# The normalisation stage of an encoder layer, written out by hand in each engine's order

## The chip, the core and the metric

The kernel runs on one core of a Trainium2 chip. A core has five engines that work side by side, each through its own queue of instructions: TensorE (PE in the profile; its loads of weights are PEld), VectorE (DVE), ScalarE (ACT), GpSimd (POOL) and SyncE (SP). They wait for each other by semaphores. Transfers between memory and the core are run by 16 DMA engines; SyncE, ScalarE and GpSimd can issue them. The metric is the device time of one execution in microseconds.

## The reference

The kernel computes one layer of a hybrid encoder (`DEPTH` is 1) on 512 tokens of width 2048, with 16 learned meta tokens ahead of them, so 528 rows in all. What the change touches is the first step, the RMS norm, and two of the column groups of the projection behind it:

```python
def rmsnorm(x, w):
    xf = x.astype(jnp.float32)
    y = xf * lax.rsqrt(jnp.mean(xf * xf, axis=-1, keepdims=True) + EPS)
    return (y * w.astype(jnp.float32)).astype(x.dtype)
...
    u = rmsnorm(h, norm_w)
    proj = u @ w_in.astype(dt_)
...
    gcode = gcode.reshape(Bsz, L, 2, GLA_RANK).astype(jnp.float32)
...
    dt = jax.nn.softplus(dt_raw.reshape(Bsz, L, 2, SSD_HEADS).astype(jnp.float32)
                         + ssd_dt_bias.astype(jnp.float32))
...
    o_gla = rmsnorm(o, gla_norm_w).astype(dt_).reshape(Bsz, L, GLA_WIDTH) * jax.nn.silu(ggate)
```

All other column groups of `proj` feed three branches (gated linear attention, differential attention, a state-space scan), whose outputs go through one output projection, a residual and a last norm.

## The kernel before, in words

The rows of the input are five blocks: `xt[4, j]` the 16 meta tokens, `xt[0, j]` to `xt[3, j]` 128 tokens each, and each block is four pieces j of 512 columns. `normalize(t)` squares the four pieces, some on ScalarE and some on VectorE, sums the squares (`ss`), takes the root on GpSimd (`r`) and scales the pieces in place. `features` then turns each of the 16 feature tiles k: transposes on TensorE into `pb`, one copy to `uh` on ScalarE (times `norm_w`), and the rest of each value, `ul`, on VectorE. A value is thus kept as two parts, so that a product of full precision is three matmuls (`uh` with `whi`, `ul` with `whi`, `uh` with `wlo`). `whi` and `wlo` are the two parts of a weight; a copy on ScalarE and a subtraction on VectorE make them.

Two groups of products stand in this stage: B, 48 matmuls for each half of the rows (`t1_half`; the first half is the blocks 4, 0, 1, the second the blocks 2, 3), and the small group of the codes and of dt, `comb` (`comb_half`), 32 for each half. There are four `pb` buffers. Behind the stage comes a chain on `comb` that gives dt and the decays (up to `Xr`), and the products of the next column tiles.

The order of before is not written by hand. The framework's scheduler takes the instructions of the whole kernel and orders them on each engine by its own model of their times; so an instruction that stands late in the source can come early in a queue. Each engine takes its queue in order. Loads use eight counters in turn: a load is issued only when the one that used its counter before, eight loads ahead, has landed.

`gn` holds the norm weights of two branches, each loaded broadcast to 128 partitions (L304, L305) and scaled on VectorE (L306, L307). It is first read 464.8 us into the span (L883).

Of the kernel before, what the change touches and what calls it, by code (L numbers as in the profile page):

```python
# [8 lines left out]
F32 = mybir.dt.float32  # L9
# [8 lines left out]
P = 128  # L18
# [24 lines left out]
def encoder_kernel(ctx, tc, x, meta, rel_bias, final_norm_w, norm_w, w_in, w_out, gla_wa2, gla_ba,  # L43
# [27 lines left out]
    def cpy(out, in_, **kw):  # L71
        nc.scalar.activation(out, in_, AF.Copy, **kw)  # L72
# [78 lines left out]

    def t1_weights(c0, nk, tag):

        out_ = []
        for k0 in range(0, KT, 8):
            raw = wpool.tile([P, 8, P], F32, name="wraw")
            nc.sync.dma_start(raw, win[:, k0:k0 + 8, c0:c0 + P])
            for i in range(0, 8, nk):
                hi = slot(tag, [P, nk, P], F32R, name="whi")
                lo = slot(tag, [P, nk, P], F32R, name="wlo")  # L160
                cpy(hi, raw[:, i:i + nk])
                tt(lo, raw[:, i:i + nk], hi.bitcast(F32), ALU.subtract)
                out_.append((hi, lo))
        return out_

    def t1_half(acc, ws, hf):
        nk = KT // len(ws)
        o, us = (acc[0][:, 0:HA], slice(0, HA)) if hf == 0 else (acc[1][:, 0:HB], slice(HA, L))
        for k in range(KT):
            hi, lo = ws[k // nk]  # L170
            for n, (wt, ur) in enumerate(((hi, uh[k]), (hi, ul[k]), (lo, uh[k]))):
                mm(nc, o, wt[:, k % nk, :], ur[:, us], k == 0 and n == 0, k == KT - 1 and n == 2)
# [73 lines left out]
    nc.tensor.transpose(pv[:, 0:92], vecs, ident[0:92, 0:92])
    nc.vector.tensor_copy(vt, pv[:, 0:92])
    nw = vt[:, 0:16]
    gba = vt[:, 88:92]

    def normalize(t):
        rows = NM if t == 4 else P
        ss = small.tile([P, 1], F32, name="ss")
        ssq = small.tile([P, 5], F32, name="ssq", bufs=5)
        nc.gpsimd.memset(ssq[:, 4:5], EPS)
        for j in range(4):
            scr = slot("w")
            if j < (2 if t < 2 else 3):
                nc.scalar.activation(scr[0:rows, 0:512], xt[t, j][0:rows], AF.Square, scale=D ** -0.5,
                                     accum_out=ssq[0:rows, j:j + 1])  # L260
            else:
                nc.vector.tensor_tensor_reduce(scr[0:rows, 0:512], xt[t, j][0:rows], xt[t, j][0:rows], 1.0 / D, 0.0,
                                               ALU.mult, ALU.add, ssq[0:rows, j:j + 1])
        nc.vector.tensor_reduce(ss[0:rows], ssq[0:rows], AX.X, ALU.add)
        r = small.tile([P, 1], F32, name="r")
        gtt(r[0:rows], ss[0:rows], mhalf[0:rows, 0:1], ALU.pow)
        for j in range(4):
            if j == 3:
                cpy(xt[t, j][0:rows], xt[t, j][0:rows], scale=r[0:rows, 0:1])
            else:  # L270
                ts_(xt[t, j][0:rows], xt[t, j][0:rows], r[0:rows, 0:1], None, ALU.mult)

    def features(parts, us):
        for k in range(KT):
            pt = pb()
            n = 0
            for t in parts:

                nc.tensor.transpose(pt[:, n:n + P], xt[t, k // 4][:, (k % 4) * P:(k % 4 + 1) * P], ident)
                n += NM if t == 4 else P  # L280
            cpy(uh[k][:, us], pt[:, 0:n], scale=nw[:, k:k + 1])
            stt(ul[k][:, us], pt[:, 0:n], nw[:, k:k + 1], uh[k][:, us].bitcast(F32), ALU.mult, ALU.subtract)
# [733 lines left out]
```

## Time and profile before

| | |
|---|---|
| median of three runs | 920.37 us (917.81 to 920.91) |
| the profiled execution | 917.57 us, span 915.8 us |
| TensorE busy | 876.9 us, 96% of the span |
| VectorE busy | 554.0 us, 60% |
| ScalarE busy | 383.7 us, 42% |
| GpSimd busy | 183.7 us, 20% |
| share of the 16 DMA engines, 0 to 12 us and 12.0 to 23.1 us | 0.82 and 1.04 |

The profiled execution is one run; its span goes from the first to the last instruction, and 1.8 us lie around it. Busy matmuls are pipelined, so that one can begin while the one before it is still counted. The stage of the change is the first 54 us or so of the span.

### The profile page before, as it was taken

To read this page: it belongs to the slowest core of one execution; us is meant where nothing else is said; L and a number is where in the kernel's file an instruction comes from. 1 tells how busy PE (TensorE), PEld (TensorE's weight loads), DVE (VectorE), ACT (ScalarE), POOL (GpSimd) and SP (SyncE) were. 2 spreads that over 40 slices of the span, in tenths; PEclk is the share of its full clock that TensorE was granted. 3 is DMA by queue.
4 is the path that set the end of the run, shared out by engine and by line. 5 is a ranking of instruction groups with operands and counts; after the bars stand their busy time and mean duration, and the time that the engine had idled before them with its cause. 6 is when DMAs were issued, how large, how long until landed. Compare 5 with 4: busy or idle time off the path is not lost.

```text
span 915.8 us, 14461 instructions
## 1 busy us (share of the span) xinstructions
PE 876.9 (96%) x5737; PEld 779.9 (85%) x5737; DVE 554.0 (60%) x1049; ACT 383.7 (42%) x753; POOL 183.7 (20%) x215
## 2 busy tenths in 40 slices
PE   3898999999999999999999999999999999999996
PEld 3898999997778888899999999988888888888884
DVE  6669977999957568853642467775552543232334
ACT  6555434335534376734232345553342333132322
POOL 2006203549246302010040000000120002020200
PEclk9999999999999999999999999999999999999998
DMA  9422332221223234123337333324223532322225
GB/s 238 106 70 69 76 87 71 64 76 46 70 72 91 79 85 115 47 70 93 87 77 203 84 82 84 85 81 136 81 81 103 173 123 90 109 92 92 93 92 184
DMA packets 99587, 88.33 MB, mean 96 GB/s; under 512 B 8223, under 2 KB 75415, under 8 KB 99519
## 3 DMA queue, kind: packets, MB, share of 16 engines
q1 hardware_dynamic: 95183, 77.06, 29.8%
q0 software_dynamic: 1456, 5.10, 1.9%
q10 hardware_dynamic: 2880, 5.24, 1.7%
q8 instruction: 45, 0.74, 0.3%
q14 instruction: 23, 0.19, 0.1%
HBM read 83.18 MB, written 6.34 MB: 98 GB/s over the span
## 4 chain that ended last, share of the span: by engine, by line
PE 75%; DVE 12%; ACT 4%; issue 4%; DMA 2%; SPq 1%; POOL 1%; ACTq 0%; POOLq 0%; DVEq 0%
PE pm L39 65%; PE pb L39 7%; DVE acc L413 2%; DVE wlo L146 2%; DMA xt<-in_x_dram 2%; PE pb L898 1%; PE pb L852 1%; DVE sg L450 1%; ACT whi L72 1%; DVE acc L411 1%; DVE xs L459 1%; DMA gn<-in_diff_norm_w_dram 1%; SPq L228 1%; DVE m L552 1%; DVE m L453 0%
## 5 line engine op out<-in xcount | busy, mean ns | idle before, releaser
L146 DVE TENSOR_TENSOR wlo<-wraw,whi 128x1024 fp32r<-128x1024 f32 (+1 forms) x128 | 163.7, 1280 | 212.6 <-ACT whi L72 212.3
L72 ACT ACTIVATE whi<-wraw 128x1024 fp32r<-128x1024 f32 (+1 forms) x134 | 137.2, 1025 | 297.6 <-PE pm L39 237.4
L39 PE MATMUL pm<-ul,whi 128*128 128x272 f32 (+2 forms) x960 | 224.4, 300 | 0.0
L39 PE MATMUL pm<-uh,whi 128*128 128x272 f32 (+2 forms) x960 | 221.9, 298 | 0.6 <-ACT uh L72 0.6
L39 PE MATMUL pm<-uh,wlo 128*128 128x256 f32 (+2 forms) x928 | 214.6, 297 | 1.2 <-DVE wlo L146 0.7
L39 PEld LDWEIGHTS pm<-uh,whi 128*128 128x128 f32 x960 | 154.8, 189 | 6.7 <-ACT uh L72 1.2
L39 PEld LDWEIGHTS pm<-ul,whi 128*128 128x128 f32 x960 | 155.0, 189 | 5.1 <-issue 0.2
L39 PEld LDWEIGHTS pm<-uh,wlo 128*128 128x128 f32 x928 | 149.7, 189 | 6.8 <-DVE wlo L146 2.1
L39 PE MATMUL pm<-wlo,uh 128*128 128x512 f32 x256 | 102.5, 401 | 2.3 <-DVE wlo L146 2.3
L39 PE MATMUL pm<-whi,ul 128*128 128x512 f32 x256 | 101.3, 397 | 0.0
L39 PE MATMUL pm<-wlo,mh 128*128 128x512 f32 x256 | 100.6, 394 | 0.0
L39 PE MATMUL pm<-whi,ml 128*128 128x512 f32 x256 | 100.5, 394 | 0.0
L39 PE MATMUL pm<-whi,uh 128*128 128x512 f32 x256 | 95.0, 398 | 0.0
L39 PE MATMUL pm<-whi,mh 128*128 128x512 f32 x256 | 90.3, 395 | 0.0
L129 POOL TENSOR_TENSOR rs_r<-rs_v,mhalf 128x1 f32<-128x1 f32 (+1 forms) x28 | 20.5, 734 | 273.2 <-DVE rs_v L128 191.9
L39 PEld LDWEIGHTS pm<-wlo,uh 128*128 128x128 f32 x256 | 48.6, 190 | 13.3 <-DVE wlo L146 2.8
L39 PEld LDWEIGHTS pm<-whi,ml 128*128 128x128 f32 x256 | 48.2, 188 | 11.4
L39 PEld LDWEIGHTS pm<-whi,ul 128*128 128x128 f32 x256 | 48.6, 190 | 10.5
L39 PEld LDWEIGHTS pm<-whi,mh 128*128 128x128 f32 x256 | 48.1, 188 | 11.1
L39 PEld LDWEIGHTS pm<-wlo,mh 128*128 128x128 f32 x256 | 48.1, 188 | 10.9
L39 PEld LDWEIGHTS pm<-whi,uh 128*128 128x128 f32 x256 | 48.2, 189 | 10.7
L932 POOL TENSOR_TENSOR hx<-hx,fw 128x512 f32<-128x512 f32 x12 | 18.1, 1537 | 164.6 <-ACT junk L919 164.6
(304 smaller groups left out, 1197.7 us busy)
## 6 DMA issues: line engine op xcount, KB each, us to landing
wraw<-in_w_in_dram SPq DMA_DIRECT2D x96, 512.0 KB, 3.9
wraw<-in_w_out_dram SPq DMA_DIRECT2D x30, 512.0 KB, 3.6
xt<-in_x_dram SPq DMA_DIRECT2D x16, 256.0 KB, 5.2
hx<-in_x_dram ACTq DMA_DIRECT2D x16, 256.0 KB, 3.9
out_dram<-hx SPq DMA_DIRECT2D x16, 256.0 KB, 2.8
tabr<-tabd POOLq DMA_DIRECT2D x4, 520.0 KB, 7.0
bt<-tabr POOLq DMA_DIRECT2D x4, 456.0 KB, 3.6
fw<-in_final_norm_w_dram ACTq DMA_DIRECT2D x4, 256.0 KB, 4.3
```

Source lines behind the costliest of these rows:

```text
L39: nc.tensor.matmul(out, lhsT=lhsT, rhs=rhs, start=start, stop=stop)
L72: nc.scalar.activation(out, in_, AF.Copy, **kw)
L129: gtt(r[0:rows, 0:cols], v[0:rows, 0:cols], mhalf[0:rows, 0:cols], ALU.pow)
L146: tt(lo, raw, hi.bitcast(F32), ALU.subtract)
L228: nc.sync.dma_start(raw[:, :, 32 * i:32 * i + 32], win[:, k0:k0 + 8, c0:c0 + 32])
L411: ts_(acc, xp[:, 0:L], cw[:, 0:1], cbb[:, j:j + 1], ALU.mult, ALU.add)
L413: stt(acc, xp[:, k:k + L], cw[:, k:k + 1], acc, ALU.mult, ALU.add)
L450: stt(sg[:, c], px[:, c * P:(c + 1) * P], Xs[:, 1, c, h:h + 1], sg[:, c], ALU.subtract, ALU.min)
L459: tt(lo, src, hi.bitcast(F32), ALU.subtract)
L552: tt(m, m, sc, ALU.mult)
L852: nc.tensor.transpose(pt[:, c * P:(c + 1) * P], w_[:, c * P:(c + 1) * P], ident)
L932: gtt(hx[t, b], hx[t, b], fw[b], ALU.mult)
```

## The change

The scheduler is switched off for the stage (`tc.manual_schedule()`): its instructions stand in each engine's queue in the order in which the new code gives them. Block 0 is squared and scaled first, the transposes run three tiles ahead of the copies, and the products of `comb` follow those of B with a lag of six tiles, and one tile in the second half. The first load of B's weights and one of `comb` stand ahead of x block 2. The identity, the meta tokens and `pick` are loaded from ScalarE's queue, `norm_w`, the conv weights and two more vectors from GpSimd's. The scaling of the meta block, of block 2 and of half of block 3 goes to GpSimd. The loads and scalings of `gn` are moved down in the source, behind the gated linear attention. What stands outside the `with` is still placed by the scheduler.

```diff
-    for t in (4, 0, 1):
-        normalize(t)
-    features((4, 0, 1), slice(0, HA))
-    comb_ps, b_ps = (pm(), pm()), (pm(), pm())
-    t1_half(b_ps, b_w, 0)
-    comb_half(comb_ps, 0)
-    for t in (2, 3):
-        normalize(t)
-    features((2, 3), slice(HA, L))
-    t1_half(b_ps, b_w, 1)
-    comb_half(comb_ps, 1)
...
+    def scale(t, j, eng):
+        rows = NM if t == 4 else P
+        ap = xt[t, j][0:rows]
+        if eng == "A":
+            cpy(ap, ap, scale=rx[t][0:rows, 0:1])
+        else:
+            (nc.vector if eng == "V" else nc.gpsimd).tensor_scalar(ap, ap, rx[t][0:rows, 0:1], None, ALU.mult)
...
+    def turn(hf, k, parts):
+
+        if (hf, k) not in pts:
+            pts[hf, k] = pb()
+        n = 0
+        for t in BL[hf]:
+            if t in parts:
+
+                nc.tensor.transpose(pts[hf, k][:, n:n + P], xt[t, k // 4][:, (k % 4) * P:(k % 4 + 1) * P], ident)
+            n += NM if t == 4 else P
+
+    def parts_of_u(hf, k):
+        us, n = US[hf], (HA, HB)[hf]
+        pt = pts[hf, k]
+        cpy(uh[k][:, us], pt[:, 0:n], scale=nw[:, k:k + 1])
+        stt(ul[k][:, us], pt[:, 0:n], nw[:, k:k + 1], uh[k][:, us].bitcast(F32), ALU.mult, ALU.subtract)
+
+    def prod_b(hf, k):
+        o = b_ps[hf][:, 0:(HA, HB)[hf]]
+        hi, lo = b_w[k // 4]
+        for n, (wt, ur) in enumerate(((hi, uh[k]), (hi, ul[k]), (lo, uh[k]))):
+            mm(nc, o, wt[:, k % 4, :], ur[:, US[hf]], k == 0 and n == 0, k == KT - 1 and n == 2)
...
+    with tc.manual_schedule():
+
+        load_x(0)
+        nc.scalar.dma_start(ident, masks[M_ID])
+        nc.vector.memset(zp, 0.0)
+        for j in range(4):
+            xt[4, j] = slot("ya", [P, 512], name="mt")
+            nc.gpsimd.memset(xt[4, j], 0.0)
+            nc.scalar.dma_start(xt[4, j][0:NM], meta[:, j * 512:(j + 1) * 512])
...
+        load_x(1)
...
+        load_b()
+        load_comb()
+        load_x(2)
+        load_comb()
+        load_b()
+        load_x(3)
...
+        LEAD = 3
+        for k in range(LEAD):
+            turn(0, k, (4, 0))
...
+        scale(0, 3, "A")
+        split_b()
+        scale(1, 0, "V")
+        scale(1, 1, "A")
+        for k in range(LEAD):
+            turn(0, k, (1,))
+        todo = [lambda: scale(1, 2, "V"), lambda: split_b(), lambda: scale(1, 3, "A"),
+                lambda: split_comb(), lambda: square(2, 0, "A"), lambda: split_b(),
+                lambda: square(2, 2, "V"), lambda: square(2, 1, "A"), lambda: square(2, 3, "V"),
+                lambda: split_b(), lambda: root(2), lambda: split_comb(),
+                lambda: [scale(2, j, "P") for j in range(4)], lambda: square(3, 0, "A"),
+                lambda: square(3, 2, "V"), lambda: square(3, 1, "A"), lambda: square(3, 3, "V"),
+                lambda: root(3), lambda: [scale(3, j, "P") for j in range(2)],
+                lambda: scale(3, 2, "V"), lambda: scale(3, 3, "A")]
+        CLAG = 6
+        for k in range(KT + CLAG):
+            if k < KT:
+                parts_of_u(0, k)
+                if k + LEAD < KT:
+                    turn(0, k + LEAD, BL[0])
+                prod_b(0, k)
+            for _ in range(2):
+                if todo:
+                    todo.pop(0)()
+            if k >= CLAG:
+                prod_comb(0, k - CLAG)
+            if k >= KT + CLAG - LEAD:
+                turn(1, k - (KT + CLAG - LEAD), BL[1])
...
@@ -300,19 +376,9 @@
...
-    gn = const.tile([P, 2, P], F32, name="gn")
-    nc.sync.dma_start(gn[:, 0], gla_norm_w.broadcast_to([P, P]))
-    nc.sync.dma_start(gn[:, 1], diff_norm_w.broadcast_to([P, P]))
-    ts_(gn[:, 0], gn[:, 0], 0.5, None, ALU.mult)
-    ts_(gn[:, 1], gn[:, 1], 1.0 - LAMBDA_INIT, 0.5, ALU.mult, ALU.mult)
...
@@ -763,6 +829,12 @@
...
+    gn = const.tile([P, 2, P], F32, name="gn")
+    nc.sync.dma_start(gn[:, 0], gla_norm_w.broadcast_to([P, P]))
+    nc.sync.dma_start(gn[:, 1], diff_norm_w.broadcast_to([P, P]))
+    ts_(gn[:, 0], gn[:, 0], 0.5, None, ALU.mult)
+    ts_(gn[:, 1], gn[:, 1], 1.0 - LAMBDA_INIT, 0.5, ALU.mult, ALU.mult)
```

What the scheduler made of it is seen in the queues of the two built programs. First VectorE of the kernel before, in the first half of the stage; `ul_143` is `ul` of feature tile 7, `ul_144` of tile 8.

```order
L282 SCALAR_TENSOR_TENSOR ul_143<-pb,vt,uh_127 128x272
L306 TENSOR_SCALAR gn<-gn 128x128
L307 TENSOR_SCALAR gn<-gn 128x128
L264 TENSOR_REDUCE ss<-ssq 128x1
L282 SCALAR_TENSOR_TENSOR ul_144<-pb,vt,uh_128 128x272
L282 SCALAR_TENSOR_TENSOR ul_145<-pb,vt,uh_129 128x272
L282 SCALAR_TENSOR_TENSOR ul_146<-pb,vt,uh_130 128x272
```

And VectorE of the changed kernel at its scalings of `gn`; `ul_99` is `ul` of tile 0, `ul_100` of tile 1, `L206` a scaling of x block 1, `L222` a split of B's weights, `L237` one of `comb`'s.

```order
L260 SCALAR_TENSOR_TENSOR ul_99<-pb,vt,uh_83 128x272
L206 TENSOR_SCALAR xt<-xt,r 128x512
L222 TENSOR_TENSOR wlo<-wraw,whi 128x512
L835 TENSOR_SCALAR gn<-gn 128x128
L836 TENSOR_SCALAR gn<-gn 128x128
L260 SCALAR_TENSOR_TENSOR ul_100<-pb,vt,uh_84 128x272
L237 TENSOR_TENSOR whi<-wraw,whi 128x8x64
L260 SCALAR_TENSOR_TENSOR ul_101<-pb,vt,uh_85 128x272
L222 TENSOR_TENSOR wlo<-wraw,whi 128x512
```

The two scalings stood behind `ul` of tile 7 and stand behind `ul` of tile 0 now. Next SyncE's queue before, from x block 3 on, with the counter for which each load waits.

```order
L86 DMA xt<-in_x_dram 128x512 [waits DMAHW1_49]
L86 DMA xt<-in_x_dram 128x512 [waits DMAHW2_49]
L86 DMA xt<-in_x_dram 128x512 [waits DMAHW3_49]
L86 DMA xt<-in_x_dram 128x512 [waits DMAHW4_49]
L298 DMA umask<-in_umask_dram 128x128 [waits DMAHW5_49]
L300 DMA row_636<-in_ssd_dt_bias_dram 128x32 [waits DMAHW6_49]
L301 DMA row_636<-in_ssd_A_log_dram 128x32 [waits DMAHW7_49]
L302 DMA row_636<-in_ssd_D_dram 128x16 [waits DMAHW0_49]
L304 DMA gn<-in_gla_norm_w_dram 128x128 [waits DMAHW1_49]
L305 DMA gn<-in_diff_norm_w_dram 128x128 [waits DMAHW2_49]
L309 DMA masks<-in_masks_dram 128x4x128 [waits DMAHW3_49]
```

The same place in the changed kernel.

```order
L181 DMA xt<-in_x_dram 128x512 [waits DMAHW0_49]
L181 DMA xt<-in_x_dram 128x512 [waits DMAHW1_49]
L181 DMA xt<-in_x_dram 128x512 [waits DMAHW2_49]
L181 DMA xt<-in_x_dram 128x512 [waits DMAHW3_49]
L374 DMA umask<-in_umask_dram 128x128 [waits DMAHW4_49]
L376 DMA row_649<-in_ssd_dt_bias_dram 128x32 [waits DMAHW5_49]
L377 DMA row_649<-in_ssd_A_log_dram 128x32 [waits DMAHW6_49]
L378 DMA row_649<-in_ssd_D_dram 128x16 [waits DMAHW7_49]
L379 DMA masks<-in_masks_dram 128x4x128 [waits DMAHW0_49]
L833 DMA gn<-in_gla_norm_w_dram 128x128 [waits DMAHW1_49]
L834 DMA gn<-in_diff_norm_w_dram 128x128 [waits DMAHW2_49]
```

The load of `gn` from `diff_norm_w` shared its counter with the second piece of x block 3, and shares it with the third now; the load of the masks stood behind it and stands ahead.

## Rows read from the trace of the kernel before

**Rows 1.** The page's busy times: engine, us, share of the span, instructions.

```profile
PE 876.9 (96%) x5737; PEld 779.9 (85%) x5737; DVE 554.0 (60%) x1049; ACT 383.7 (42%) x753; POOL 183.7 (20%) x215
```

**Rows 2.** Windows: stretch in us, busy us and instructions by engine, clock, DMA, GB/s.

```profile
core 0: us, PE busy (x) PEld busy (x) DVE busy (x) ACT busy (x) POOL busy (x), PEclk, DMA share, GB/s
...
12.00:23.10 11.10, 8.82 (x35) 7.16 (x36) 9.81 (x28) 8.48 (x20) 1.45 (x4) 1.00 1.04 246
0.00:30.80 30.80, 14.21 (x78) 12.36 (x78) 18.58 (x56) 20.14 (x53) 6.74 (x24) 1.00 0.88 223
30.80:53.45 22.65, 21.93 (x180) 21.31 (x180) 13.22 (x29) 12.23 (x28) 0.37 (x3) 1.00 0.26 68
70.00:80.00 10.00, 7.14 (x55) 6.60 (x53) 9.53 (x13) 3.33 (x6) 6.23 (x5) 1.00 0.08 24
222.00:231.30 9.30, 6.46 (x27) 4.70 (x26) 9.30 (x12) 4.28 (x11) 9.14 (x6) 1.00 0.09 34
231.30:234.80 3.50, 3.50 (x11) 2.69 (x10) 3.50 (x10) 1.89 (x3) 0.35 (x1) 0.51 0.55 157
```

**Rows 3.** The chain of waits, 0 to 54 us: start, us, what.

```profile
18.22 5.96 DMA xt<-in_x_dram
24.20 5.88 DMA gn<-in_diff_norm_w_dram
```

**Rows 4.** Timeline of VectorE: start, us, instruction, idle before and its releaser.

```profile
17.92 0.49 DVE L282 SCALAR_TENSOR_TENSOR ul<-pb,vt,uh 128x272 fp32r<-128x272 f32 x1
...
26.87 0.50 DVE L282 SCALAR_TENSOR_TENSOR ul<-pb,vt,uh 128x272 fp32r<-128x272 f32 x1
27.28 0.22 DVE L306 TENSOR_SCALAR gn<-gn 128x128 f32<-128x128 f32 x1
30.10 0.23 DVE L307 TENSOR_SCALAR gn<-gn 128x128 f32<-128x128 f32 x1 [2.59 <-DMA gn<-in_diff_norm_w_dram]
```

**Rows 5.** Timeline of TensorE, around its first rise of clock and its wait.

```profile
22.07 0.43 PE L39 MATMUL pm<-uh,whi 128*128 128x272 f32 x1
...
23.27 0.29 PE L39 MATMUL pm<-uh,whi 128*128 128x272 f32 x1
...
30.85 0.33 PE L279 MATMUL pb<-masks,mt 128*128 128x128 f32 x1 [2.36 <-DVE ul L282]
```

**Rows 6.** Timeline of SyncE's queue: start and us of an issue.

```profile
23.21 0.33 SPq L304 DMA_DIRECT2D gn<-in_gla_norm_w_dram  x1
24.20 0.33 SPq L305 DMA_DIRECT2D gn<-in_diff_norm_w_dram  x1
24.84 0.38 SPq L309 DMA_DIRECT2D masks<-in_masks_dram  x1
```

**Rows 7.** Time from issue to landing of the two loads of `gn`.

```profile
DMA to landing us min/median/max: 3.3/4.6/5.9
```

**Rows 8.** Groups of VectorE, 0 to 54 us: busy us, mean ns, idle before.

```profile
L282 DVE SCALAR_TENSOR_TENSOR ul<-pb,vt,uh 128x272 fp32r<-128x272 f32 x16 | 7.4, 495 | 1.2 <-ACT uh L72 1.2
...
L262 DVE CUSTOM_DVE_ANT_0 w<-xt 128x512 f32<-128x512 f32 x6 | 4.0, 682 | 0.3 <-DMA xt<-in_x_dram 0.2
L162 DVE TENSOR_TENSOR wlo<-wraw,whi 128x512 fp32r<-128x512 f32 x4 | 2.7, 679 | 0.0
```

**Rows 9.** Groups of GpSimd over the whole span.

```profile
L883 POOL TENSOR_TENSOR od<-od,gn 128x512 f32<-128x512 f32 x4 | 5.2, 1298 | 2.1 <-DVE od L866 2.1
...
L266 POOL TENSOR_TENSOR r<-ss,mhalf 128x1 f32<-128x1 f32 x4 | 2.6, 661 | 17.8 <-DVE ss L264 17.8
...
L106 POOL MEMSET mt<- 128x1024 f32 x2 | 1.8, 950 | 0.3 <-POOLq L1002 0.3
```

**Rows 10.** Waits of TensorE over the whole span: us, times, longest.

```profile
PE pb L39 <- DVE Xr L388: 2.9, 1, 2.9
```

More of the change, by code (lines that the diff above doesn't have):

```diff
@@ L150, in encoder_kernel @@
     wout = w_out.rearrange("o (k p) c -> p (o k) c", p=P)
[L152 to L172, printed above, removed]
     def t1(cols, tokens=True):
@@ new lines, in square, with root @@
+    def square(t, j, eng):
+        rows = NM if t == 4 else P
+        scr = slot("w")
+        if eng == "A":
+            nc.scalar.activation(scr[0:rows, 0:512], xt[t, j][0:rows], AF.Square, scale=D ** -0.5,
+                                 accum_out=ssq[t][0:rows, j:j + 1])
+        else:
+            nc.vector.tensor_tensor_reduce(scr[0:rows, 0:512], xt[t, j][0:rows], xt[t, j][0:rows], 1.0 / D, 0.0,
+                                           ALU.mult, ALU.add, ssq[t][0:rows, j:j + 1])
+    def root(t):
+        rows = NM if t == 4 else P
+        ss = small.tile([P, 1], F32, name="ss")
+        nc.vector.tensor_reduce(ss[0:rows], ssq[t][0:rows], AX.X, ALU.add)
+        rx[t] = small.tile([P, 1], F32, name="r")
+        gtt(rx[t][0:rows], ss[0:rows], mhalf[0:rows, 0:1], ALU.pow)
@@ L248, in encoder_kernel @@
[L248 to L282, printed above, removed]
-    for t in (4, 0, 1):
-        normalize(t)
@@ new lines, in prod_comb @@
+    def prod_comb(hf, k):
+        o = comb_ps[hf][:, 0:(HA, HB)[hf]]
+        for n, ur in enumerate((uh[k], ul[k])):
+            mm(nc, o, comb_w[k // 8][:, k % 8, :], ur[:, US[hf]], k == 0 and n == 0, k == KT - 1 and n == 1)
+    vecs = slot("st", [92, P], name="vecs")
+    pks = slot("w", [P, 32], name="pks")
+    with tc.manual_schedule():
+        load_x(0)
+        nc.scalar.dma_start(ident, masks[M_ID])
+        nc.vector.memset(zp, 0.0)
+        for j in range(4):
+            xt[4, j] = slot("ya", [P, 512], name="mt")
+            nc.gpsimd.memset(xt[4, j], 0.0)
+            nc.scalar.dma_start(xt[4, j][0:NM], meta[:, j * 512:(j + 1) * 512])
+        nc.gpsimd.memset(mhalf, -0.5)
+        nc.vector.memset(warm, 0.0)
+        nc.scalar.activation(warm, warm, AF.Exp)
+        load_x(1)
+        for t in range(5):
+            ssq[t] = small.tile([P, 5], F32, name="ssq", bufs=5)
+            nc.gpsimd.memset(ssq[t][:, 4:5], EPS)
+        nc.gpsimd.dma_start(vecs[0:16], norm_w.rearrange("o (k p) -> (o k) p", p=P))
+        nc.gpsimd.dma_start(vecs[16:76], conv_w.rearrange("o k (j p) -> (o k j) p", p=P))
+        nc.gpsimd.dma_start(vecs[76:88], conv_b.rearrange("o (j p) -> (o j) p", p=P))
+        nc.gpsimd.dma_start(vecs[88:92].rearrange("h (z k) -> h z k", z=2),
+                            gla_ba.rearrange("o z (h k) -> (o h) z k", h=4))
+        load_b()
[4 more added lines that the diff above has]
+        load_x(3)
+        cpy(XE, zp[0:96, 0:8].rearrange("p a b -> p (a b)"))
+        cpy(BE, vz[0][0:96])
+        cpy(RB, vz[0][0:96, 0:4])
+        square(0, 0, "A")
+        square(0, 2, "V")
+        square(0, 1, "A")
+        square(0, 3, "V")
+        root(0)
+        nc.scalar.dma_start(pks, pick.rearrange("p z h -> p (z h)"))
+        pv = pb()
+        nc.tensor.transpose(pv[:, 0:92], vecs, ident[0:92, 0:92])
+        square(4, 0, "A")
+        square(4, 2, "V")
+        square(4, 1, "A")
+        square(4, 3, "V")
+        root(4)
+        nc.vector.tensor_copy(vt, pv[:, 0:92])
+        scale(0, 0, "V")
+        scale(0, 1, "A")
+        scale(0, 2, "V")
+        for j in range(4):
+            scale(4, j, "P")
+        LEAD = 3
+        for k in range(LEAD):
+            turn(0, k, (4, 0))
+        square(1, 0, "A")
+        square(1, 2, "V")
+        square(1, 1, "A")
+        square(1, 3, "V")
+        root(1)
+        scale(0, 3, "A")
[26 more added lines that the diff above has]
+                turn(1, k - (KT + CLAG - LEAD), BL[1])
+        for k in range(KT):
+            parts_of_u(1, k)
+            if k + LEAD < KT:
+                turn(1, k + LEAD, BL[1])
+            prod_b(1, k)
+            if k >= 1:
+                prod_comb(1, k - 1)
+        prod_comb(1, KT - 1)
```

84 lines of the change are left out of this document (38 added, 46 removed).

## Prediction

> **What bounds the kernel now.** I read the page first. TensorE is busy for 96% of the span [rows 1], so what a change is worth is the time in which TensorE has no product to run, or runs at half speed. The windows put most of that at the start: in the first 30.8 us TensorE issues 78 matmuls, and in the next 22.65 us it issues 180, one each 0.126 us [rows 2]. This first part is the normalisation stage. The chain of waits says what ends last there: the load of a piece of x, and right behind it the load of `gn` from `diff_norm_w`, which lands 5.88 us after its issue, at 30.08 [rows 3]. Nothing in this stage needs `gn`. The timeline of VectorE shows why it counts all the same: the scaling of `gn` stands in VectorE's queue between `ul` of feature tile 7 and `ul` of tile 8, VectorE takes its instructions in order, and it stands idle there for 2.59 us until the load lands [rows 4]. TensorE starts again at 30.85, after 2.36 us, with `ul` as its releaser [rows 5].
>
> **The change, part by part.** *What bears on nothing.* The same squares, splits, transposes and 160 products are run; so their own time is the same, and only their order and their waits are to be priced. The loads of meta tokens, identity, vectors and `pick` leave SyncE's queue. I cost that at nothing: the DMA engines are full while x comes in (share 1.04 from 12.0 to 23.1 [rows 2]), so the bytes in front of the last pieces of x take the same time. The price if that cover were gone stands with the rivals.
>
> *Where `gn` stands now.* The source moves `gn` far down, but the built program does not: its two scalings stand in VectorE's queue behind `ul` of tile 0 and ahead of `ul` of tile 1. In the trace of before VectorE had done eight `ul` when it met the load; now it will have done one. I take VectorE to be there at about 20 us: its first `ul` starts at 17.92 in before [rows 4], and one scaling and one split follow. When exactly doesn't matter as long as `gn` is later. Behind the two rows wait `ul` 1 to 15, the other splits, and the squares of x blocks 2 and 3; behind those waits TensorE. ScalarE has the like: its `ea` (from `A_log`) now stands ahead of `uh` of tile 1, but `A_log` is issued three loads ahead of the first `gn`, so that ScalarE is free first, and I charge nothing for it.
>
> *Term 1, products not done when the wait ends.* Up to `ul` of tile 1 TensorE's new order has 20 matmuls: one for the vectors, fifteen transposes (tiles 0 to 4), three products of tile 0 and the first of tile 1. In before 78 are done by 30.8 [rows 2]. The 58 that are missing cost 58 x 0.126 = 7.3 us, at the pace of before from 30.8 to 53.45 [rows 2].
>
> *Term 2, when the wait ends.* A load is issued when the one eight places ahead of it has landed. In before the second `gn` load waits in this way for the second piece of x block 3 and is issued at 24.20, just as that lands (18.22 + 5.96) [rows 3, 6]. Now it waits for the third piece of that block, and the load of four masks (256 KB) stands ahead of it instead of behind: 24.5 is my estimate for its issue, since issues there are 0.6 us apart (24.20, 24.84 [rows 6]) and the bytes ahead are the same. The two `gn` loads of before took 3.3 and 5.9 us to land [rows 7]. So it lands between 24.5 + 3.3 = 27.8 and 24.5 + 5.9 + 1.1 = 31.5 (1.1 for the masks, 256 KB at the 246 GB/s of [rows 2]): -2.3 to +1.4 us against 30.08. I take 29.5, so -0.6, near the longer of the two, which is the same load.
>
> *Term 3, TensorE's clock.* Until about 23.1 TensorE ran at half speed (products 0.43 us at 22.07, 0.29 at 23.27 [rows 5]), though the granted clock reads 1.00 there, which I take to mean that nothing was recorded before its first rise. After its wait of 2.36 us it came back at full speed: the transpose at 30.85 takes 0.33 [rows 5]. Later, behind a stretch in which it was busy for 6.46 of 9.3 us, the granted clock is 0.51 for 3.5 us, the lower level (1.2 GHz) [rows 2]. In the new order TensorE stands nearly still for some 9 us before 30. Below: nothing, as after 2.36 us. Above: half speed for 6 us, about the denser part of the slow stretch of before, so 3.0 us lost. I take the row that is nearest, 3.5 us at half speed: +1.8.
>
> *Term 4, scalings on GpSimd.* All four pieces of x block 2 and two of block 3 are now scaled on GpSimd, and `scale(3, 2)` on VectorE, which needs GpSimd's root of block 3, stands ahead of `ul` of tile 10. From the release VectorE has nine `ul` (0.495), four splits (0.68) and four squares (0.68) before it [rows 8], 10 us. Block 2's root needs ten of these (5.9) and 0.66 for itself; then come four scalings. GpSimd's rows hold no scaling by one operand: a memset of 128 x 1024 takes 0.95, so 0.48 for 512 columns, and a product of two operands at 128 x 512 takes 1.3 [rows 9]. Four are 1.9 or 5.2 us, so block 3's root, 0.66 more, is ready 10.7 or 12.4 us after the release: VectorE waits 0.7 to 2.4 us. TensorE, slow at first, is itself not at tile 10 much before; 0 to 3.0, and I take +1.0. The Trainium skill (GPSIMD Engine Reference, Engine selection) says that an elementwise operation with one input runs at roughly line rate there; by that the four would cost near the memset's time, the wait would be 0.7, and the sum 0.5 us smaller. No run here shows it yet.
>
> *Term 5, behind the stage.* The rest of the order is nearly that of before, so the delay is carried through: from 53 us on TensorE is fed by what it has just made. One wait could give something back: TensorE stands 2.9 us for `Xr` [rows 10], 70 to 80 us [rows 2], and now nine more products stand ahead of that place: 0 to -1.1. I take -0.5.
>
> *Sum.* 7.3 - 0.6 + 1.8 + 1.0 - 0.5 = +9.0. The profiled execution took 917.57 (span 915.8), which gives 926.6. The median of the three runs is 920.37, 2.8 above it; by that the sum would be 929.4. I predict 928.0, in the middle. The lower bounds give 7.3 - 2.3 + 0 + 0 - 1.1 = +3.9, so 921.5; the upper ones 7.3 + 1.4 + 3.0 + 3.0 + 0 = +14.7, so 932.3, or 935.1 by the median.
>
> **The rivals.**
> *A, faster: the `gn` loads land before VectorE gets to them.* Then nothing stands still at 20 us, and TensorE runs its remaining 243 matmuls from 19.5: 243 x 0.126 + 1.8 = 32.4, an end of the stage at 51.9. Before it ends at 53.45, with six fewer of the next tile's products done, so 54.2 on the same count: -2.3 us, 915.3 by the profiled execution or 918.1 by the median. It decides if `gn` lands by about 21 (30.1 less the 9.0). For it speaks that SyncE has seven loads fewer to issue; against it, that the last pieces of x land at 24 us with full DMA engines [rows 2, 3], and `gn` is issued behind them.
> *B, three queues bring the data earlier.* SyncE's seven loads took it at most some 2.7 us (seven at 0.38, the longer of the single issues of [rows 6]). If issue were what x waits for, x and `gn` would land that much earlier, and the sum would be 9.0 - 2.7 = +6.3, 923.9 to 926.7. The DMA share of 1.04 speaks against it. The Trainium skill (DMA: Bandwidth & Descriptors, Issuing engines are not separate DMA queues) says that loads of all engines run on the same 16 DMA engines and that several issuers save issue time only; by that B gives nothing.
> *C, no change:* the late start is made good by the wait at 70 to 80, where VectorE is the busy one (9.53 of 10 us [rows 2]). At most 2.9 of the 9.0 can go so; together with the lower bounds +2, 920 to 922.
>
> **How the numbers follow.** About 0.3% of this kernel (2.8 us) is what a measurement can tell from no change. My forecast, the wait at `gn` with its terms: 0.78, all of it slower. B: 0.09, slower too in most of its width. C: 0.06, most of it within 0.3%. A: 0.07; its -2.3 alone would stand within 0.3%, and faster counts where the clock is also up early, so I give 0.05 to faster and the rest to no change. That gives faster 0.05, same 0.08, slower 0.87. The range runs from the lower bound, 921.5, to 933.0, between the two upper ones; A and part of C are left out.
>
> **What would show it.** VectorE idle behind the first `ul`, from about 20 to 27.8 or more, with the load of `gn` as releaser; some 20 matmuls until then; products of 0.4 us behind it; the last `comb` product at 60 to 64 instead of 53.45; GpSimd's scalings at 0.5 to 1.3 us. I am wrong if `gn` lands by 21, or if TensorE has 60 or more matmuls done by 30.8.

## The result, and the profile after

The changed kernel takes 930.39 us (median of four runs, 930.18 to 930.52), the kernel before 920.55 (four runs, 917.81 to 920.91): a ratio of 1.0113, 95% interval 1.0094 to 1.0133, so slower by 9.8 us. The prediction was 928.0, slower. The profiled execution took 930.52, with a span 12.8 us longer than that of before. Before's profiled run lay some 3 us under its median, so the spans differ by more than the medians do.

The page first; the second line answers to [rows 1], and what has grown is GpSimd.

```profile
span 928.6 us, 14462 instructions
...
PE 878.2 (95%) x5737; PEld 781.4 (84%) x5737; DVE 551.2 (59%) x1045; ACT 383.0 (41%) x747; POOL 206.0 (22%) x231
```

Windows of the changed kernel, columns as in [rows 2] (the third pair is VectorE, the fifth GpSimd, and the granted clock stands behind them).

```profile
0.00:30.80 30.80, 5.57 (x20) 4.14 (x20) 10.39 (x34) 14.99 (x38) 15.68 (x31) 1.00 0.83 228
...
40.00:45.00 5.00, 0.76 (x8) 0.56 (x6) 0.90 (x2) 0.97 (x2) 4.90 (x6) 1.00 0.00 0
45.57:48.98 3.41, 3.41 (x18) 3.41 (x17) 1.63 (x5) 1.29 (x3) 2.00 (x4) 0.50 0.02 5
...
30.80:68.20 37.40, 33.15 (x243) 32.85 (x244) 20.59 (x47) 16.59 (x37) 11.81 (x11) 0.95 0.14 37
```

Until 30.8 TensorE has 20 matmuls where it had 78 [rows 2]: the wait at `gn`, as forecast. But there is a second hole, 40 to 45, in which GpSimd alone is busy, and behind it 3.4 us at a granted clock of 0.50. VectorE's timeline (compare [rows 4]) has both waits.

```profile
23.58 0.50 DVE L260 SCALAR_TENSOR_TENSOR ul<-pb,vt,uh 128x272 fp32r<-128x272 f32 x1 [1.09 <-ACT uh L72]
...
28.59 0.23 DVE L835 TENSOR_SCALAR gn<-gn 128x128 f32<-128x128 f32 x1 [3.52 <-DMA gn<-in_gla_norm_w_dram]
30.12 0.23 DVE L836 TENSOR_SCALAR gn<-gn 128x128 f32<-128x128 f32 x1 [1.30 <-DMA gn<-in_diff_norm_w_dram]
30.27 0.49 DVE L260 SCALAR_TENSOR_TENSOR ul<-pb,vt,uh 128x272 fp32r<-128x272 f32 x1
...
44.03 0.48 DVE L206 TENSOR_SCALAR xt<-xt,r 128x512 f32<-128x512 f32 x1 [4.57 <-POOL r L198]
```

TensorE's timeline, to be read against [rows 5] and [rows 10]:

```profile
30.81 0.59 PE L39 MATMUL pm<-ul,whi 128*128 128x272 f32 x1 [4.18 <-DVE ul L260]
31.20 0.43 PE L39 MATMUL pm<-uh,wlo 128*128 128x272 f32 x1
...
35.95 0.29 PE L39 MATMUL pm<-uh,wlo 128*128 128x272 f32 x1
...
44.98 0.39 PE L39 MATMUL pm<-ul,whi 128*128 128x272 f32 x1 [4.24 <-DVE ul L260]
...
68.14 0.28 PE L39 MATMUL pm<-ul,whi 128*128 128x256 f32 x1
...
92.74 1.19 PE L39 MATMUL pb<-Xr,pkr 128*128 128x512 f32 x4 [1.41 <-DVE Xr L454]
```

TensorE starts again at 30.81 (before 30.85), its products take 0.43 there and 0.29 at 35.95, and the stage's last product starts at 68.14. The last line is the product behind the chain on `comb`, with the wait that was 2.9 [rows 10]. Its start serves as a mark below; before has it at 79.01.

```profile
79.01 1.19 PE L39 MATMUL pb<-Xr,pkr 128*128 128x512 f32 x4 [2.86 <-DVE Xr L388]
```

The mark is the same product in every kernel, but not the same amount of work lies ahead of it. The windows of before and of after up to the mark:

```profile
0.00:79.01 79.01, 58.84 (x443) 55.77 (x443) 53.70 (x117) 45.50 (x102) 16.71 (x35) 1.00 0.50 127
0.00:92.74 92.74, 61.84 (x453) 59.52 (x453) 51.95 (x114) 45.07 (x96) 37.42 (x51) 0.98 0.40 108
```

Before and its variants (e3, e8, e11) have 443 or 444 matmuls ahead of the mark, after and its variants 452 or 453 (e4 and e12 their added ones besides). Nine or ten more are some 1.2 us at the 0.126 of the prediction. So between after and its variants marks compare directly; against before they overstate the loss by 1.2.

GpSimd's timeline in the changed kernel, and its groups from 0 to 60 us (busy us, mean ns):

```profile
13.99 7.45 POOL L206 TENSOR_SCALAR mt<-mt,r 16x512 f32<-16x512 f32 x4
21.41 0.56 POOL L198 TENSOR_TENSOR r<-ss,mhalf 128x1 f32<-128x1 f32 x1
...
36.59 6.70 POOL L206 TENSOR_SCALAR xt<-xt,r 128x512 f32<-128x512 f32 x4
...
43.43 0.57 POOL L198 TENSOR_TENSOR r<-ss,mhalf 128x1 f32<-128x1 f32 x1
```

```profile
L206 POOL TENSOR_SCALAR xt<-xt,r 128x512 f32<-128x512 f32 x6 | 10.1, 1699 | 0.2
L206 POOL TENSOR_SCALAR mt<-mt,r 16x512 f32<-16x512 f32 x4 | 7.4, 1869 | 0.1
```

Four scalings stand ahead of the root of block 1, and four ahead of the root of block 3. The first four hold block 1 until 22; the others hold VectorE from 39.5 to 44 and TensorE with it.

### The profile page after: what moved, and what is told of

It is laid out like the page before. It is cut to its first block, busy times and chain, and to the rows that moved or that the text cites. A ratio compares the mean times of both kernels' runs of the same rounds, so it can differ in the third digit from the quotient of the medians.

```text
span 928.6 us, 14462 instructions
## 1 busy us (share of the span) xinstructions
PE 878.2 (95%) x5737; PEld 781.4 (84%) x5737; DVE 551.2 (59%) x1045; ACT 383.0 (41%) x747; POOL 206.0 (22%) x231
## 4 chain that ended last, share of the span: by engine, by line
PE 70%; DVE 10%; ACT 4%; issue 3%; DMA 2%; POOL 1%; ACTq 0%; POOLq 0%; DVEq 0%
PE pm L39 61%; PE pb L39 7%; DVE wlo L116 3%; DMA wraw<-in_w_in_dram 2%; DVE acc L479 1%; PE pb L924 1%; PE pb L970 1%; ACT whi L72 1%; DVE xs L525 1%; DVE acc L477 1%; DVE m L618 1%; DVE sg L516 0%; ACT L682 0%; ACT gt L679 0%; DVE acc L482 0%
## 5 line engine op out<-in xcount | busy, mean ns | idle before, releaser
L39 PE MATMUL pm<-uh,whi 128*128 128x272 f32 (+2 forms) x960 | 226.6, 301 | 0.4 <-ACT uh L72 0.4
L39 PEld LDWEIGHTS pm<-whi,uh 128*128 128x128 f32 x256 | 48.0, 188 | 10.5
```

What stands on the lines that cost most here:

```text
L39: nc.tensor.matmul(out, lhsT=lhsT, rhs=rhs, start=start, stop=stop)
```

## The experiments

The kernels of one group ran on the same chip beside runs of before, whose medians were 920.55 (with the changed kernel), 921.23 (the first four experiments), 920.86 (the next four) and 919.19 (the last four). Sizes are read from the mark, the start of the `Xr` product in each trace; the ratio is to before on the same chip. A mark is that of one execution, and stretches in which the granted clock is 0.50 fall ahead of it in some traces and not in others: for some 3.4 us in after, e1, e7 and e11, for 6.4 to 6.8 in e4, e6 and e13, none in the others. A difference of a few tenths between marks says nothing.

| kernel | us | ratio (95%) | mark |
|---|---|---|---|
| before | 920.55 | | 79.01 |
| after | 930.39 | 1.0113 (1.0094 to 1.0133) | 92.74 |
| e1_gn_early | 932.01 | 1.0112 (1.0091 to 1.0132) | 93.82 |
| e2_x_scales_off_gpsimd | 927.19 | 1.0060 (1.0042 to 1.0079) | 89.04 |
| e3_before_gn_early | 920.90 | 0.9995 (0.9979 to 1.0010) | 80.18 |
| e4_turns_repeated | 930.69 | 1.0097 (1.0078 to 1.0115) | 93.35 |
| e6_gn_late | 928.30 | 1.0085 (1.0059 to 1.0111) | 90.90 |
| e7_gn_late_no_pool_scales | 921.43 | 1.0004 (0.9991 to 1.0018) | 83.73 |
| e8_before_gn_filled | 917.01 | 0.9961 (0.9942 to 0.9980) | 76.81 |
| e9_e7_meta_rows | 920.22 | 0.9995 (0.9976 to 1.0013) | 82.26 |
| e10_gn_late_x_scales | 924.89 | 1.0068 (1.0050 to 1.0086) | 86.66 |
| e11_before_gn_late | 916.98 | 0.9971 (0.9958 to 0.9985) | 78.59 |
| e12_x_scales_turns | 927.92 | 1.0097 (1.0081 to 1.0113) | 88.81 |
| e13_meta_scales_only | 925.51 | 1.0069 (1.0053 to 1.0086) | 86.96 |

### gn loaded early (e1, e3): no answer, but a price

```diff
+        nc.gpsimd.dma_start(gn[:, 0], gla_norm_w.broadcast_to([P, P]))
+        nc.gpsimd.dma_start(gn[:, 1], diff_norm_w.broadcast_to([P, P]))
...
-    nc.sync.dma_start(gn[:, 0], gla_norm_w.broadcast_to([P, P]))
-    nc.sync.dma_start(gn[:, 1], diff_norm_w.broadcast_to([P, P]))
```

> After with one thing moved: the two gn loads are issued from GpSimd's queue right behind the vectors, and gn is scaled on VectorE behind the last product of the stage. Theory (VectorE stands at gn until 30.1 with all that feeds TensorE behind it): VectorE's second ul moves from 30.27 to about 26, TensorE's release from 30.81 to about 26.5, since the next late thing is ScalarE's ea at 25.4; about -4.3 against after, some 926. The part that remains of the lateness then comes from the scalings on GpSimd, whose waits of 4.2 to 4.6 us must be there unchanged, some 4 us earlier. Rival (gn only happens to be there; x or the clock is what is waited for): within 0.5 us of after.

> Before with the two gn loads issued from GpSimd's queue ahead of the vectors, and gn scaled there. Theory (the wait at gn in VectorE's queue held up the stage in before too, 2.59 us on VectorE and 2.36 on TensorE): -2.4 against before, 915 to 918, the 60th to 78th matmul follow without the gap. Rival (in before the wait at gn is hidden: TensorE would have waited for x block 3's squares in any case): 0, 920.

Neither gained; by the ratios both rivals' numbers came (e1's median is 1.6 us above after's, its mark 1.1 later). The timeline of ScalarE in e1 says why that settles nothing:

```profile
28.83 0.23 ACT L433 ACTIVATE ea<-row 128x32 f32<-128x32 f32 x1 [3.47 <-DMA row<-in_ssd_A_log_dram]
```

After has this `ea`, which waits for the load of `A_log`, at 25.38. Two loads of 64 KB, issued from GpSimd's queue ahead of x blocks 2 and 3, put off what was loaded behind them by about 3.4 us; by 246 GB/s [rows 2] they should take 0.5. The rows of GpSimd's queue, 0 to 32 us, in e1 and then in after (packets, MB, share of the 16 engines), show most of it:

```profile
q0 software_dynamic: 224, 0.18, 7.5%
q0 software_dynamic: 160, 0.05, 0.7%
```

The 6.8% between them are 2.2 us of all 16 engines. The wait at `gn` was gone, and `ea` took its place 3.4 us later than it stood. The edit took away one thing and added another of like size. In e3 it is the same: SyncE begins to issue x blocks 2 and 3 at 17.39 us, in before at 15.49.

### gn out of the stage altogether (e6)

```diff
         prod_comb(1, KT - 1)
+        nc.gpsimd.dma_start(gn[:, 0], gla_norm_w.broadcast_to([P, P]))
+        nc.gpsimd.dma_start(gn[:, 1], diff_norm_w.broadcast_to([P, P]))
+        ts_(gn[:, 0], gn[:, 0], 0.5, None, ALU.mult)
+        ts_(gn[:, 1], gn[:, 1], 1.0 - LAMBDA_INIT, 0.5, ALU.mult, ALU.mult)
```

> After with gn's two loads issued from GpSimd's queue behind its last scaling of the stage, and gn scaled behind the stage's last product, so that neither the load nor the scaling stands in the stage at all (e1_gn_early put 3 us of transfers ahead of x and so could not tell). Theory (VectorE's wait at gn is what releases the stage): the second ul at about 26.2 instead of 30.27, held then by ScalarE's ea at 25.4; -4 against after, about 926.4; the 4.2 to 4.6 us wait for GpSimd's scalings stays and comes 4 us earlier. Rival, from e1_gn_early (something else is late by 30 anyway): within 0.5 us of after, 930.

TensorE and VectorE of e6:

```profile
26.78 0.59 PE L39 MATMUL pm<-uh,whi 128*128 128x272 f32 x1 [1.04 <-ACT uh L72]
27.31 0.60 PE L39 MATMUL pm<-ul,whi 128*128 128x272 f32 x1
```

```profile
26.76 0.50 DVE L260 SCALAR_TENSOR_TENSOR ul<-pb,vt,uh 128x272 fp32r<-128x272 f32 x1 [1.54 <-ACT uh L72]
...
41.75 0.49 DVE L206 TENSOR_SCALAR xt<-xt,r 128x512 f32<-128x512 f32 x1 [4.56 <-POOL r L198]
```

VectorE's second `ul` starts 3.5 us earlier (26.76, not 30.27), and so does TensorE's product with it (27.31, not 30.81), nearly as expected. But VectorE then waits 1.0 us for ScalarE's `whi`, the wait for GpSimd's root ends only 2.3 earlier, and the mark moves by 1.8. The rest may be the clock, which falls within that wait and stays low for twice as long as in after:

```profile
40.40:47.10 6.70, 4.40 (x20) 4.40 (x21) 2.87 (x7) 2.83 (x6) 6.02 (x9) 0.50 0.06 9
```

The wait at `gn` is real; taken away alone it gives a quarter of what I gave it.

### The scalings of x off GpSimd (e2), and with gn late (e10)

```diff
-                lambda: [scale(2, j, "P") for j in range(4)], lambda: square(3, 0, "A"),
+                lambda: [scale(2, j, "VAVA"[j]) for j in range(4)], lambda: square(3, 0, "A"),
...
-                lambda: root(3), lambda: [scale(3, j, "P") for j in range(2)],
+                lambda: root(3), lambda: [scale(3, j, "VA"[j]) for j in range(2)],
```

> After with the six scalings of x blocks 2 and 3 that stand on GpSimd given to VectorE and ScalarE in turn; the wait for gn stays. Theory (GpSimd's 1.7 us for each of them set a wait of 4.2 us at 41 to 45 and sent TensorE's clock down a second time, 3.4 us at half speed): that wait goes, -4.2, and the second fall with it, -1.7, less about 1 for the work that VectorE and ScalarE take over: -4 to -6 against after, 924.5 to 926.5. Rival (my term 4 as on record, +1.0 for these scalings): -1.0, about 929.4.

> After with gn late as in e6_gn_late and the six scalings of x blocks 2 and 3 off GpSimd as in e2_x_scales_off_gpsimd, while the four scalings of the meta block stay on GpSimd. e6 gave -2.1, e2 -3.2, and e7, which also moved the meta block's four, -9.0. Theory 1 (the waits simply add; the meta block's scalings, which hold block 1 until 21.4, are the missing 3.7): -5 to -6, about 925. Theory 2 (gn and GpSimd's scalings of x hide each other, and each alone gives too little; the meta block's scalings are hidden by ea at 25.4): -8 to -9, about 922.

In e2 the mark moves by 3.7 us (the median by 3.2); TensorE's wait of 4.24 us is gone, and its longest behind the release is

```profile
38.22 0.39 PE L39 MATMUL pm<-uh,whi 128*128 128x272 f32 x1 [1.25 <-ACT uh L72]
```

Term 4 as on record (1.0 us) is out. In e10 the mark moves by 6.1, near the sum of e6 and e2 (1.8 + 3.7). The median is lower by 5.5 than after's, the ratio by 0.0045 (4.1 us): theory 1, within what the ratios can tell.

### The meta block's scalings off GpSimd (e13), and all of it (e7)

```diff
-            scale(4, j, "P")
+            scale(4, j, "VAVA"[j])
```

> After with only the meta block's four scalings moved from GpSimd to VectorE and ScalarE. Block 1's factor is then ready at about 17 instead of 21.4. Theory (what lies ahead of the wait for gn is hidden by it, so nothing earlier than 30 counts): 9 to 12 more matmuls can't run, since they stand behind ul of tile 1; 0 to -0.5, about 930. Rival (it frees VectorE and ScalarE for work of the later tiles, or brings the release forward): -2 or more.

> After with gn as in e6_gn_late and all ten scalings on GpSimd (meta block, x blocks 2 and 3) given to VectorE and ScalarE in turn. Theory (the two waits account for the lateness and add): -4 for gn and -3.2 (as e2_x_scales_off_gpsimd measured) or a little more, so -7 to -9 against after, 921.5 to 923.5, within 3 us of before; TensorE has no wait over 2 us behind its release at 26. Rival (they don't add: one wait covers the other): -4 to -5, 925.5 to 926.5.

e13's theory was wrong: the mark moved by 5.8 us, the median by 4.9. VectorE's timeline shows that more than the scalings changed:

```profile
20.07 0.50 DVE L260 SCALAR_TENSOR_TENSOR ul<-pb,vt,uh 128x272 fp32r<-128x272 f32 x1 [1.09 <-ACT uh L72]
...
24.22 0.50 DVE L260 SCALAR_TENSOR_TENSOR ul<-pb,vt,uh 128x272 fp32r<-128x272 f32 x1
...
27.03 0.23 DVE L835 TENSOR_SCALAR gn<-gn 128x128 f32<-128x128 f32 x1 [1.71 <-DMA gn<-in_gla_norm_w_dram]
28.99 0.23 DVE L836 TENSOR_SCALAR gn<-gn 128x128 f32<-128x128 f32 x1 [1.74 <-DMA gn<-in_diff_norm_w_dram]
```

Block 1 is ready 3.5 us earlier (first `ul` at 20.07, not 23.58), and the scheduler, which still places `gn`, put it behind four `ul` instead of one. So e13 is both effects together. The clean step is from e10 to e7, which have `gn` late alike: 2.9 us at the mark for the meta block's four scalings. That is rather too little, since e7's trace has 3.4 us at a granted clock of 0.50 ahead of the mark (33.5 to 36.9) and e10's has none; by the medians the step is 3.5, by the ratios 5.9 (3.8 to 8.0). e7 is 9.0 below after by the mark and by its median, and level with before. The groups of VectorE and ScalarE in e7, 0 to 60 us, give the price of the same scalings there:

```profile
L206 DVE TENSOR_SCALAR xt<-xt,r 128x512 f32<-128x512 f32 x8 | 3.6, 478 | 0.4 <-POOL r L198 0.3
L206 DVE TENSOR_SCALAR mt<-mt,r 16x512 f32<-16x512 f32 x2 | 0.9, 471 | 0.1
```

```profile
L72 ACT ACTIVATE xt<-xt,r 128x512 f32<-128x512 f32 x8 | 5.6, 715 | 3.2 <-POOL r L198 3.2
```

### TensorE kept busy through the wait (e4, e12)

```diff
+                if k == 0:
+                    for _ in range(8):
+                        turn(0, 4, BL[0])
```

> After with the three transposes of tile 4 ahead of the gn wait run nine times instead of once (24 transposes more, into the same place), so that TensorE is busy from about 24.8 to 30 where it stood still. Theory of the clock (after a stretch nearly without work TensorE comes back at half speed and loses some 2.2 us to 35.3): the products behind the release take the shorter time from the start or from a point well ahead of 35.3, -1 to -2 against after, about 928.5 to 929.5. Rival (the slow start has nothing to do with what TensorE did before): 0, or up to +1.5 if the transposes run past the release.

> e2_x_scales_off_gpsimd with the 24 transposes more of e4_turns_repeated, so that TensorE comes out of the gn wait at full speed and no wait for GpSimd's scalings follows that could swallow the gain. Theory (the slow start costs what the shorter products save, 4.5 us at half speed): -1.5 to -2.2 against e2, 925 to 925.7. Rival (VectorE and ScalarE set the pace behind the release, not TensorE): within 0.5 of e2, 927.

The edit does what it should: the product behind the release takes 0.39 us instead of 0.59. It buys nothing. In e12 the mark is 0.2 us ahead of e2's, and its time is not lower. The window of e12 from 29.8, and then that of e2 from 30.1, where its products take 0.43 us and not 0.29 (the clock column reads 1.00 there all the same, as in before until 23.1), show the reason:

```profile
29.80:34.50 4.70, 3.90 (x24) 3.07 (x24) 4.70 (x14) 2.20 (x5) 0.00 (x0) 1.00 0.04 11
```

```profile
30.10:34.60 4.50, 4.46 (x20) 4.46 (x21) 4.50 (x11) 2.07 (x5) 0.00 (x0) 1.00 0.03 8
```

VectorE (third pair) is busy for the whole of both stretches. It sets the pace behind the release, and TensorE, at half speed busy for 4.46 of 4.50 us, nearly keeps up with it. In e4 GpSimd's wait follows, of 4.24 us again (TensorE's timeline):

```profile
30.32 0.39 PE L39 MATMUL pm<-ul,whi 128*128 128x272 f32 x1 [1.57 <-DVE ul L260]
...
44.49 0.59 PE L39 MATMUL pm<-ul,whi 128*128 128x272 f32 x1 [4.24 <-DVE ul L260]
```

Behind it comes a window at half speed twice as long as after's:

```profile
43.60:50.40 6.80, 5.91 (x26) 5.92 (x27) 3.15 (x7) 2.76 (x6) 3.47 (x4) 0.50 0.00 0
```

That is 3.4 us more at half speed, and the mark comes 0.6 later although the wait for GpSimd ends 0.5 earlier: there the low clock is on the path, as far as one trace of each can tell.

### What else is late, and gn in the kernel before (e9, e8, e11)

In e9 the meta tokens' loads move to GpSimd's queue, and `dt_bias`, `A_log`, `D` and the copy of `pick` move behind the stage's work; the loads of `umask` and of four masks, which stood among them, now follow x block 3 directly.

> e7 with three things more: the meta tokens loaded from GpSimd's queue so that ScalarE's table load and squares don't stand behind its own loads, the loads of dt_bias, A_log and D issued behind the stage's work on GpSimd, and the copy of pick behind the stage, so that neither ea nor pick stands in ScalarE's way. Theory (what is left of the lateness is ScalarE's late start and ea at 25.4): block 0 and 1 normalised by about 16.5, TensorE running on from about 19 without a wait over 2 us, the last product of the stage near 51 against 53.5 in before; -11 to -14 against after, 917 to 919.5, 2 to 4 below before. Rival (the landing of x block 3 at 24.8 and its squares set the pace, so an early start is lost again): no better than before, 921 to 923.

The mark is 1.5 us earlier than e7's, and the time is no better than before's: the rival's result. From 24 to 32 us, e9 and then before:

```profile
24.00:32.00 8.00, 5.46 (x33) 4.06 (x33) 6.40 (x16) 6.27 (x17) 1.11 (x2) 1.00 0.71 189
```

```profile
24.00:32.00 8.00, 5.64 (x48) 5.42 (x47) 4.75 (x15) 4.72 (x14) 1.36 (x5) 1.00 0.77 174
```

VectorE and ScalarE are busy for some 80% of it and TensorE gets 33 matmuls, while before runs 48 with both of them less busy: in the new order each tile's products wait for their own `uh` and `ul` among splits, squares and scalings. e9's mark is still 3.3 us behind before's, 2.1 without the nine products; whether this order is the whole of that was not tried by itself.

For before, e8 leaves the loads and scalings of `gn` out (GpSimd fills it with 0.5, so its output is not the layer's), and e11 issues them behind the first half of `comb`:

```diff
+    nc.gpsimd.tensor_copy(gr[:, 0:2, 0:1], comb[:, 0:2, None])
+    nc.gpsimd.dma_start(gr[:, 0], gla_norm_w.broadcast_to([P, P]))
+    nc.gpsimd.dma_start(gr[:, 1], diff_norm_w.broadcast_to([P, P]))
+    nc.gpsimd.tensor_copy(gn[:, 0:2, 0:1], comb[:, L - 2:L, None])
+    ts_(gn[:, 0], gr[:, 0], 0.5, None, ALU.mult)
+    ts_(gn[:, 1], gr[:, 1], 1.0 - LAMBDA_INIT, 0.5, ALU.mult, ALU.mult)
```

> Before with gn filled with 0.5 by GpSimd: the two loads and two scalings of gn are left out (the norm weights of two branches are then constants). Theory (VectorE's 2.59 us at gn held TensorE in before too, and e3_before_gn_early gained nothing only because the transfers of gn then stood ahead of x, whose last piece landed 2 us later): -2.4 against before, about 918.5. Rival (in before the wait at gn is hidden, or is given back at the wait for Xr): within 0.5 us of before, 921.

> Before with gn's loads issued from GpSimd's queue once the first half of the comb product is done and gn scaled into a second tile once the second half is done; nothing is left out. Theory (the wait at gn and its transfers cost before 3.9 us, as e8_before_gn_filled showed by leaving gn out): -3 to -4 against before, 917 to 918, the fastest of all. Rival (the two scalings and a one-column copy on GpSimd land in the stretch at 70 to 80 where VectorE is the busy engine, or the late load is waited for there): 0 to -1.

Both are faster than before, by 3.9 us (1.8 to 5.3) and by 2.2 to 2.7 (interval 1.4 to 3.9). In their traces TensorE's wait of 2.36 us at 30.85 is gone, and 103 (e8) and 108 (e11) matmuls are done by 30.8 us, against 78. So the wait at `gn` did cost before about what [rows 4, 5] show; e8 gained more than the 2.4 of the wait, with the transfers gone too. e11 leaves nothing out and is the fastest full version here. Its mark is only 0.4 us ahead of before's: its profiled run is its slowest (919.58; its runs go down to 914.33), with 3.4 us at a granted clock of 0.50 from 34.7 on, behind a wait of 2.21 us for `uh`.

Behind the mark the two orders differ too. In the traces of e3, e8 and e11 the granted clock falls to 0.50 behind the wait of 2.9 us for `Xr`; in before's own trace it does not (e8, then before):

```profile
76.00:83.00 7.00, 6.19 (x33) 5.82 (x34) 6.19 (x13) 4.42 (x12) 1.98 (x2) 0.76 0.30 77
76.00:83.00 7.00, 4.14 (x31) 3.81 (x30) 6.67 (x14) 5.45 (x13) 0.23 (x1) 1.00 0.19 50
```

From the mark to the end of the span e3, e8 and e11 take 838.1 to 839.2 us, before 836.8, and after and its variants, whose wait for `Xr` is 1.4, 835.4 to 837.5, without such a fall and with nine products less to do. A likely reading is that most runs of before have this fall and its profiled run does not, which would be part of the 3 us between that run and the median, and part of why e9 is level with before although its mark is later. No trace of a usual run of before is kept, so this is not shown.

## Why the prediction was right, and where it was not

The direction and the mechanism at its head held: VectorE stands behind its first `ul` with the load of `gn` as releaser, 20 matmuls are done, the products behind it take 0.43. Three signs were off: VectorE comes to `gn` at 25, not 20, GpSimd's scalings take 1.7 to 1.9 us, not 0.5 to 1.3, and the stage ends at 68.14, not 60 to 64.

**Terms 1 and 2.** 20 matmuls against 78, and TensorE's restart at 30.81 against 30.85: 7.3 us, and 0 instead of -0.6. As an account of the trace this is exact. As a cause it is not: with `gn` out of the way (e6) only 1.8 us come back. "When exactly doesn't matter as long as `gn` is later" was true of the time and hid the cause: VectorE got to its first `ul` at 23.58 and not at 20, because block 1's root stood behind the meta block's four scalings on GpSimd, and ScalarE's `ea` stood at 25.4, so much of the 7.3 was late without `gn`.

**Terms 3 and 4.** From 30.8 to 68.2 the 243 matmuls took 37.4 us; at the 0.126 of term 1 they take 30.6. The 6.8 between them answer to terms 3 and 4, for which I had 2.8. The failed step is term 4, 1.0 (0 to 3.0): the six scalings cost 3.7 (e2), more than its upper bound. The path it described was right: with the measured 1.70 us for a scaling of 128 x 512 its own working gives 5.9 + 0.66 + 4 x 1.70 + 0.66 = 14.0 us, a wait of 4.0, and VectorE waited 4.57. The price of a scaling was wrong. Its bounds were two rows, a memset and a product of two operands of 1.30 us [rows 9]. The same view of before has dearer operations of that shape, one of them an addition at 1.73, with which the longest wait would have been 4.1, and the upper bound would have held:

```profile
L543 POOL TENSOR_TENSOR ya<-ya,yo 128x512 f32<-128x512 f32 x14 | 24.3, 1732 | 47.1 <-DVE yo L542 47.1
```

The Trainium skill (GPSIMD Engine Reference, Engine selection) has elementwise operations with one input at roughly line rate; here they took 3.6 times as long as on VectorE (478 ns), so the measurement decides against it. (By that rule, the prediction says, its sum would be 0.5 us smaller; by its own wait of 0.7 in place of 1.0 it is 0.3.) The same mistake stands in "their own time is the same": ten scalings moved to an engine that needs three to four times as long as VectorE, and the meta block's four (2.9 us or more) had no price at all.

Term 3 (+1.8) was wrong in its place: the slow products behind the release cost hardly anything (0.2 us between e2 and e12), since VectorE sets the pace there. A second fall of the clock, behind GpSimd's wait, was not foreseen; it does cost (e4), and goes with the wait (e2, whose trace has no fall ahead of the mark). The 3.1 us of the 6.8 that e2 does not give back were not taken apart; 2.0 of them can be seen behind e2's release, where 20 matmuls fill 4.5 us, at VectorE's pace and not at 0.126.

**Term 5** was -0.5 (0 to -1.1); the wait for `Xr` went from 2.86 to 1.41 us, so -1.45, outside its bounds. Term by term, 7.3 + 6.8 - 1.45 = +12.65 against 12.8 of the spans and 12.5 at the mark without the products that moved ahead of it: the account closes, with terms 3 and 4 some 4 us larger than on record. That 928.0 came within 2.4 us of the time is in part luck: the sum of 9.0 was 3.8 short of what the profiled runs differ by, and nearly right by the medians (9.8) only because before's usual run is 3 us slower than its profiled one.

**The rivals.** A (`gn` lands by 21) and C did not happen. For B, that three queues bring the data earlier, SyncE's queue in after has

```profile
24.14 0.33 SPq L834 DMA_DIRECT2D gn<-in_diff_norm_w_dram  x1
```

against 24.20 [rows 6]: nothing came earlier. Instead ScalarE stood behind its own loads, from 2.66 to 7.5:

```profile
2.66 4.85 ACTq L284 DMA_DIRECT2D mt<-in_meta_tokens_dram  x4
7.53 1.28 ACT L287 ACT_TABLE_LOAD   x1 [7.53 <-DMA xt<-in_x_dram]
```

Before has its table load at the start, and ScalarE's first square at 7.38 us, where after has it at 9.75:

```profile
0.74 1.28 ACT L90 ACT_TABLE_LOAD   x1 [0.74 <-PEq L1002]
```

**The sum of causes.** At the mark the change costs 13.7 us, or 12.5 without the products that now stand ahead of it. Out of these come 1.8 with `gn` alone, 6.1 with the scalings of x too (e10), 9.0 with the meta block's as well (e7), 10.5 with ScalarE's loads, `ea` and `pick` (e9). What is left, 3.3 or 2.1 without those products, belongs to the written order and the placing of the other loads; which part of it is open.

## What to carry to other kernels

An instruction moved to another engine is a new instruction: where no row shows it there, the two nearest rows are no bounds (the dearest row of its shape is a better one), and an instruction behind which a short one waits (here a root of 0.6 us behind four scalings) is priced with all that waits for that short one. A wait in the trace says who was last, not what is won without it: take it away together with the one next behind, as e6, e10 and e7 do step by step. A load that is needed late has to be issued late by a real dependence (e11); moving its line down in the source left its load where it was (issued at 24.14 us, in before at 24.20), and loading it early cost as much as the wait.

## What was not expected of the hardware

GpSimd's scaling by one operand takes 1699 ns for 128 x 512 and 1869 ns for 16 x 512: the number of partitions hardly counts. With one operand it is slower than the two-operand product of rows 9 (1298 ns); operations of two operands on 128 x 512 in before's trace take 1251 to 1732. What makes the scaling so slow was not tried. The two broadcast loads of `gn`, 64 KB each, put off what stood behind them by about 3.4 us when GpSimd's queue issued them (e1), over six times what their bytes take at the rate at which x came in. Whether the broadcast or the queue makes them dear was not tried.
